# Four steps instead of three per mLSTM chunk: where the state's product and the output's norm stand

## The chip, the cores and the metric

One core of a Trainium2 chip. The time is the device time of one execution in microseconds; a version is timed in several runs and the median counts. One further execution is recorded by the hardware profiler, and all rows come from it. Engines: PE (TensorE, matmul and transpose), DVE (VectorE), ACT (ScalarE), POOL (GpSimd), and SP, whose queue issues the DMAs.

## The reference, cut to what matters

A decoder layer over 1024 tokens: three token mixers on one normalised input, gates that merge them, an output projection, then a gated MLP. The change is in the second mixer, an mLSTM with 4 heads of 128, worked in 8 chunks of 128 tokens:

```python
def step(carry, inp):                       # one chunk, c_st and n_st carried
    ...
    s = jnp.einsum('bhtd,bhsd->bhts', qc, kc) * jnp.exp(log_d - m_t[..., None])
    num = s @ vc + w_inter * (c_st @ qc)    # written as einsums
    den = jnp.sum(s, axis=-1) + w_inter * (n_st @ qc)
    h = num / jnp.maximum(jnp.abs(den), jnp.exp(-m_t))
    c_new = decay * c_st + einsum('bhs,bhsv,bhsk->bhvk', wk, vc, kc)
    n_new = decay * n_st + einsum('bhs,bhsk->bhk', wk, kc)
# then per head: y_ml = sigmoid(ml_o) * rmsnorm(h) * ml_g_out
```

All values are float32.

## The kernel before, in words

Most of the time is dense projections in three matmuls of split float32 (`mm3`, L149 to L151), 128x512 each. In the stretch of the change the dense work is a list of units (`seven`, L679), each with two weight pages: the first from the tag `raw` (L688, 2 buffers), the second from the tag `pg` (L691). The tag `pg` has 16 pages; 12 of them hold the split inputs `gd` that every unit reads (L761), which leaves 4. `go(1)` (L929) lets the dense list advance by one piece. The pieces go round: the start of a new unit (24 matmuls), the end of the one before (24), the middle of the new one (36).

The mLSTM chunks are worked between those pieces. `ml_chunk(g, c, state)` (L841) does one chunk for two heads (`g` is 0 or 1) and is a generator whose `yield`s mark its steps. In the loop over chunks (L947) each turn takes the first step of both groups of the new chunk, one dense piece, the last step of the old chunk and the second step of the new one, and another dense piece.

- First step: loads of q, k and v into `y` (L846, L850), of the output gate `og` (L852), of the gate rows `me` (L855); the causal mask on POOL (L858); the exponentials `dt_` on ACT (L864) and the scaled queries `qt` on POOL (L865); scores `pz` on PE (L868), multiplied into `dt_` on DVE (L869); k transposed on PE into `pk` (L874) and scaled on DVE into `kw` (L877); and the state's product `pst` = kw x v on PE (L880).
- Second step: numerators and denominators `pn` on PE (L887, L888), the state's update on DVE (L896), the denominators on DVE (L903 to L906), the numerators divided on ACT into `hm`, which is the first half of the tile `me` (L911), their squares (L913), and the norm: L155 on DVE, a power on POOL (L157), L916 on DVE.
- Third step: transposes `py` on PE (L920), the output gate on DVE (L922), the store (L923).

Buffers: `me` and `y` have 2, `mw` (og, dt_, qt, kw, yn) has 8. The PSUM tags `tr` (pk, pn, py) and `z` (pz, pst) have 2 banks each; the dense work uses two other tags in this stretch.

The order on each engine, SP's queue included, is fixed before the run by a planner: the place in the program is the priority, and among what its own estimate of times holds to be ready, the earliest goes first. Each engine then works its list in order and waits where a result or a buffer is late.

Of the kernel before, what the change touches and what calls it, by code (L numbers as in the profile page):

```python
# [12 lines left out]
AF = mybir.ActivationFunctionType  # L13
ALU = mybir.AluOpType
# [4 lines left out]
P = 128  # L19
# [23 lines left out]
def tile_hybrid_layer(ctx: ExitStack, tc: tile.TileContext, xT, memT, vecs, w_t, w_n, w_kv, w_if,  # L43
# [4 lines left out]
    nc = tc.nc  # L48
# [19 lines left out]
    def T(shape, tag, dt=F32, bufs=None):  # L68
        pool = {"mw": mlp, "mst": mlp, "ga": mlp, "gm": mlp,  "px": late[0]}.get(tag, sb)
        return pool.tile(shape, dt, tag=tag, name=nm(tag), bufs=bufs or BUFS[tag])  # L70

    def page(tag="pg", dt=F32):
        return T([P, S], tag, dt)
# [15 lines left out]
    def bank(tag):  # L89
        if tag in ("pj", "pv"):  # L90
            return ps.tile([P, HALF], F32, tag=tag, name=nm("ps_" + tag), bufs=2)
        if px1 is not None:
            if not spare.get(tag):
                t = two(tag)
                spare[tag] = [t[:, 1], t[:, 0]]
            return spare[tag].pop()
        return psx[0].tile([P, HALF], F32, tag=tag, name=nm("ps_" + tag), bufs=2)
# [7 lines left out]
    def ts(t):  # L105
        return slice(t * P, (t + 1) * P)
# [6 lines left out]
    ident = ident_r.bitcast(F32)  # L113
# [724 lines left out]

        return seven(w_t[T_MLO + j], w_t[T_MLO + j + 1], gx, done)

    def ml_chunk(g, c, state):  # L841
        hd = (2 * g, 2 * g + 1)
        qv = T([P, 4 * P + 258], "y")
        qk = qv[:, :4 * P].rearrange("p (i h t) -> p i h t", i=2, h=2)
        for i in range(2):
            nc.sync.dma_start(qk[:, i], qk_d[4 * i + 2 * g:4 * i + 2 * g + 2, :, ts(c)].rearrange("h p t -> p h t"))  # L846
        q, k = qk[:, 0], qk[:, 1]
        vx = qv[:, 4 * P:].rearrange("p (h v) -> p h v", h=2)
        nc.gpsimd.memset(vx[:, :, 128:129], 1.0)
        nc.sync.dma_start(vx[:, :, :P], v_d[c, :, 256 * g:256 * g + 256].rearrange("p (h v) -> p h v", h=2))  # L850
        og = T([P, 2, P], "mw")
        nc.sync.dma_start(og, o_d[2 * g:2 * g + 2, :, ts(c)].rearrange("h p t -> p h t"))  # L852
        me = T([P, 2, 2, P], "me")
        for i in range(2):
            nc.sync.dma_start(me[:, i].rearrange("p h t -> p (h t)"),  # L855
                              me_d[i, 4 * c + 2 * g:4 * c + 2 * g + 2].rearrange("h t -> (h t)")
                              .partition_broadcast(P))
        nc.gpsimd.affine_select(out=me[:, 0], in_=me[:, 0], pattern=[[0, 2], [-1, P]], compare_op=ALU.is_ge,  # L858
                                fill=-1e30, base=0, channel_multiplier=1)
        dt_ = T([P, 2, P], "mw")  # L860
        qt = T([P, 2, P], "mw")
        for i, h in enumerate(hd):
            r = 4 * c + h
            nc.scalar.activation(dt_[:, i], me[:, 0, i], AF.Exp, bias=cols[:, 0, r:r + 1])  # L864
            nc.gpsimd.tensor_mul(qt[:, i], q[:, i], me[:, 1, i])  # L865
        pz = bank("z")
        for i in range(2):
            nc.tensor.matmul(pz[:, ts(i)], k[:, i], q[:, i], start=True, stop=True)  # L868
        nc.vector.tensor_mul(dt_.rearrange("p h t -> p (h t)"), dt_.rearrange("p h t -> p (h t)"), pz[:, :2 * P])  # L869
        if c > 0:  # L870
            kw = T([P, 2, P], "mw")
            pk = bank("tr")
            for i, h in enumerate(hd):
                nc.tensor.transpose(pk[:, ts(i)], k[:, i], ident)  # L874
            for i, h in enumerate(hd):
                r = 4 * c + h
                nc.vector.tensor_scalar(kw[:, i], pk[:, ts(i)], cols[:, 1, r:r + 1], None, op0=ALU.mult)  # L877
            pst = bank("z")
            for i, h in enumerate(hd):
                nc.tensor.matmul(pst[:, i * 129:(i + 1) * 129], kw[:, i], vx[:, i], start=True, stop=True)  # L880
        yield
        pn = bank("tr")
        first = state[0] is None
        for i, h in enumerate(hd):
            o_ = pn[:, i * 129:(i + 1) * 129]
            if not first:
                nc.tensor.matmul(o_, qt[:, i], state[0][:, i], start=True, stop=False)  # L887
            nc.tensor.matmul(o_, dt_[:, i], vx[:, i], start=first, stop=True)  # L888
        if c > 0:
            new = T([P, 2, 129], "mst", bufs=2) if first else state[0]  # L890
            for i in range(2):
                s_ = pst[:, i * 129:(i + 1) * 129]
                if first:
                    nc.vector.tensor_copy(new[:, i], s_)
                else:
                    nc.vector.scalar_tensor_tensor(new[:, i], new[:, i], me[:, 1, i, 0:1], s_,  # L896
                                                   op0=ALU.mult, op1=ALU.add)
            state[0] = new

        pn2 = pn[:, :258].rearrange("p (h v) -> p h v", h=2)  # L900
        rd = small(2)
        r0 = 4 * c + 2 * g
        nc.vector.scalar_tensor_tensor(rd, pn2[:, :, 128], -1.0, cols[:, 2, r0:r0 + 2],  # L903
                                       op0=ALU.mult, op1=ALU.max)
        nc.vector.tensor_tensor(rd, rd, pn2[:, :, 128], op=ALU.max)
        nc.vector.reciprocal(rd, rd)  # L906
        ss = small(2)
        yn = T([P, 2, P], "mw")
        hm = me[:, 0]
        for i in range(2):  # L910
            nc.scalar.activation(hm[:, i], pn2[:, i, :P], AF.Copy, scale=rd[:, i:i + 1])  # L911
        for i in range(2):
            nc.scalar.activation(yn[:, i], hm[:, i], AF.Square, accum_out=ss[:, i:i + 1])  # L913
        rr = rstd_cols(ss, 2, MLD)
        for i in range(2):
            nc.vector.tensor_scalar(yn[:, i], hm[:, i], rr[:, i:i + 1], None, op0=ALU.mult)  # L916
        yield
        py = bank("tr")
        for i in range(2):
            nc.tensor.transpose(py[:, ts(i)], yn[:, i], ident)  # L920
        for i, h in enumerate(hd):
            nc.vector.scalar_tensor_tensor(og[:, i], py[:, ts(i)], col(C_GOUT + h), og[:, i], op0=ALU.mult, op1=ALU.mult)  # L922
        nc.sync.dma_start(y_d[1][2 * g:2 * g + 2, :, ts(c)].rearrange("h p t -> p h t"), og)  # L923
        yield
# [18 lines left out]
    next(rows_step)  # L943
    go(12)
    state = [[None], [None]]
    old = []
    for c in range(NCH - 1, -1, -1):  # L947
        new = [ml_chunk(g, c, state[g]) for g in range(2)]
        for u in new:
            next(u)  # L950
        go(1)
        for u in old:
            next(u)
        for u in new:
            next(u)
        go(1)
        old = new
    for u in old:
        next(u)


    def xa_attn(h):
# [67 lines left out]
    for i in range(3 * KT):  # L1030
        b, n = i // KT, i % KT
# [371 lines left out]
```

## Time and profile before

| | us |
|---|---|
| median of 3 runs | 1709.09 |
| lowest, highest | 1708.9, 1711.78 |
| the profiled execution | 1707.22 |
| its span in the trace | 1705.4 |

The profiled execution is 1.87 us below the median. Between its time and its span lie 1.8 us that the trace does not cover. PE is busy for 1666.4 us of the span. Idle time of an engine counts only where nothing else fills the span, so here the idle time of PE is what to look at, and in the stretch of the chunks above all.

### The profile page before, as it was taken

The numbers are of one execution on the slowest core, as the hardware profiler recorded it, in microseconds if no ns is written. First come the engines' busy times: TensorE is split into PE (matmuls) and PEld (weight loads), VectorE is DVE, ScalarE is ACT, GpSimd is POOL, SyncE is SP. The second block draws the span as 40 slices with busy tenths as digits, with TensorE's granted clock in tenths as the row PEclk, the third lists the DMA queues.
The fourth block names the chain that finished last, engine by engine and source line by source line (L and its number), as shares of the span: only waits on it lengthen the run. The fifth ranks groups of instructions, "written<-read, shape, count | busy, mean of one in ns | idle before, by whom it ended". The sixth has DMA issues, their size and how long they took to land.

```text
span 1705.4 us, 21424 instructions
## 1 busy us (share of the span) xinstructions
PE 1666.4 (98%) x7927; PEld 1334.5 (78%) x7927; DVE 1195.2 (70%) x1752; ACT 824.4 (48%) x1293; POOL 72.0 (4%) x149
## 2 busy tenths in 40 slices
PE   8999999999999999999999999999999999999999
PEld 4777777787777777777787888688888888788887
DVE  5558777678945555555457747997877787689874
ACT  4547667545544444555412324465554555543531
POOL 1000000020000222100000000000000000000000
PEclk9999999999999999999999999999999999999999
DMA  8321011233323545432666255142222222486042
GB/s 297 139 64 32 26 38 56 98 114 123 125 105 130 166 151 177 155 99 93 236 202 187 88 194 204 32 142 74 75 100 86 75 75 72 145 338 227 30 144 76
DMA packets 99069, 212.73 MB, mean 125 GB/s; under 512 B 13184, under 2 KB 41088, under 8 KB 98964
## 3 DMA queue, kind: packets, MB, share of 16 engines
q1 hardware_dynamic: 98964, 211.35, 36.5%
q8 instruction: 63, 1.03, 0.3%
q14 instruction: 42, 0.34, 0.1%
HBM read 156.71 MB, written 54.61 MB: 124 GB/s over the span
## 4 chain that ended last, share of the span: by engine, by line
PE 58%; DMA 2%; DVE 2%; ACT 2%; issue 1%; POOL 0%; POOLq 0%; SPq 0%; ACTq 0%; DVEq 0%
PE ps_pj L149 8%; PE ps_pj L151 8%; PE ps_pj L150 8%; PE ps_pv L150 4%; PE ps_pv L149 4%; PE ps_pv L151 4%; PE ps_tr L149 3%; PE ps_tr L150 3%; PE ps_tr L151 3%; PE ps_z L150 2%; PE ps_z L149 2%; PE ps_z L151 2%; DMA raw<-y_d 1%; PE ps_z L1003 1%; PE ps_z L978 1%
## 5 line engine op out<-in xcount | busy, mean ns | idle before, releaser
L150 PE MATMUL ps_pj<-h,whi 128*128 128x512 f32 x620 | 243.4, 393 | 0.0
L136 ACT ACTIVATE whi<-raw 128x512 fp32r<-128x512 f32 (+1 forms) x112 | 93.6, 836 | 189.2 <-PE ps_pj L150 86.2
L149 PE MATMUL ps_pj<-h,whi 128*128 128x512 f32 x412 | 163.4, 397 | 0.7 <-DVE U L1046 0.7
L149 PE MATMUL ps_pj<-pg,whi 128*128 128x512 f32 x396 | 155.2, 392 | 0.1
L151 PE MATMUL ps_pj<-pg,wlo 128*128 128x512 f32 x380 | 148.3, 390 | 0.2 <-DVE wlo L137 0.2
L150 PEld LDWEIGHTS ps_pj<-h,whi 128*128 128x128 f32 x620 | 116.5, 188 | 24.5 <-issue 1.0
L151 PE MATMUL ps_pj<-h,wlo 128*128 128x512 f32 x332 | 131.3, 395 | 0.7 <-DVE wlo L137 0.7
L816 DVE SCALAR_TENSOR_TENSOR y<-U,vec,y 128x1023 f32<-128x1023 f32 x88 | 112.4, 1279 | 8.0 <-ACT y L814 8.0
L422 DVE TENSOR_TENSOR_SCAN U<-U 128x512 f32<-128x512 f32 (+3 forms) x96 | 88.6, 964 | 31.3 <-ACT U L415 30.4
L149 PEld LDWEIGHTS ps_pj<-h,whi 128*128 128x128 f32 x412 | 77.4, 188 | 17.0 <-DVE U L1046 1.5
L137 DVE TENSOR_TENSOR wlo<-raw,whi 128x1024 fp32r<-128x1024 f32 x54 | 66.0, 1222 | 33.5 <-ACT whi L136 33.5
L149 PEld LDWEIGHTS ps_pj<-pg,whi 128*128 128x128 f32 x396 | 74.3, 188 | 17.3 <-issue 1.6
L151 PEld LDWEIGHTS ps_pj<-pg,wlo 128*128 128x128 f32 x380 | 71.3, 188 | 15.6 <-DVE wlo L137 0.6
L136 ACT ACTIVATE whi<-pg 128x512 fp32r<-128x512 f32 (+1 forms) x59 | 43.4, 737 | 75.1 <-PE ps_pv L150 20.1
L151 PEld LDWEIGHTS ps_pj<-h,wlo 128*128 128x128 f32 x332 | 62.6, 189 | 15.1 <-DVE wlo L137 1.6
L150 PE MATMUL ps_pj<-pg,whi 128*128 128x512 f32 x188 | 74.4, 396 | 0.0
L137 DVE TENSOR_TENSOR whi<-raw,whi 128x512 fp32r<-128x512 f32 x58 | 40.1, 691 | 35.7 <-ACT whi L136 35.6
L150 PE MATMUL ps_pv<-h,whi 128*128 128x512 f32 x164 | 63.8, 389 | 0.0
L814 ACT ACTIVATE y<-U,vec 128x1024 f32<-128x1024 f32 x44 | 54.6, 1241 | 14.5 <-DVE U L720 14.4
L151 PE MATMUL ps_pj<-h,whi 128*128 128x512 f32 x156 | 61.4, 393 | 0.0
L436 ACT ACTIVATE y<-ps_tr 128x1024 f32<-128x1024 f32 (+3 forms) x48 | 39.0, 813 | 39.0 <-PE ps_tr L434 38.7
L137 DVE TENSOR_TENSOR wlo<-raw,wlo 128x512 fp32r<-128x512 f32 x58 | 40.0, 690 | 24.1 <-ACT wlo L136 23.9
(429 smaller groups left out, 4328.0 us busy)
## 6 DMA issues: line engine op xcount, KB each, us to landing
raw<-in_w_t_dram SPq DMA_DIRECT2D x29, 512.0 KB, 4.4
gate_d<-U SPq DMA_DIRECT2D x24, 512.0 KB, 3.2
U<-gate_d SPq DMA_DIRECT2D x24, 512.0 KB, 3.8
pg<-in_w_up_dram SPq DMA_DIRECT2D x22, 512.0 KB, 4.0
act_d<-y SPq DMA_DIRECT2D x22, 512.0 KB
pg<-in_w_t_dram SPq DMA_DIRECT2D x21, 512.0 KB, 3.6
raw<-in_w_dn_dram SPq DMA_DIRECT2D x18, 512.0 KB, 4.7
raw<-in_w_o_dram SPq DMA_DIRECT2D x16, 512.0 KB, 3.4
```

Source lines behind the costliest of these rows:

```text
L136: nc.scalar.activation(hi, src, AF.Copy)
L137: (eng or nc.vector).tensor_sub(lo, src, hi.bitcast(F32))
L149: nc.tensor.matmul(out, lh, rh, start=start, stop=False, skip_group_check=more)
L150: nc.tensor.matmul(out, lh, rl, start=False, stop=False, skip_group_check=more)
L151: nc.tensor.matmul(out, ll, rh, start=False, stop=stop, skip_group_check=more)
L422: nc.vector.tensor_tensor_scan(f[:, a, 1:w + 1], f[:, a, 1:w + 1], f[:, a, 1:w + 1], 1.0 if o == 0 else f[:, a, 0:1], op0=ALU.mult, op1=AL ...
L436: nc.scalar.activation(wt[:, :, :w], pt[:, :, :w], AF.Copy)
L814: nc.scalar.activation(out, u, AF.Identity, bias=bias, scale=taps[0])
L816: nc.vector.scalar_tensor_tensor(out[:, :S - s], u[:, s:], taps[s], out[:, :S - s], op0=ALU.mult, op1=ALU.add)
L978: nc.tensor.matmul(z[:, i * NMEM:(i + 1) * NMEM], q[:, ts(2 * t2 + i)], kv[:, 0], start=True, stop=True)
L1003: nc.tensor.matmul(pv, kv[:, 1, ts(m)], pTs[m], start=(m == 0), stop=(m == 1))
```

## The change: what it does

- The state's product (`pst`, L878 to L880) moves from the first step into the second, behind `pn` and ahead of the state's update.
- The second step ends behind the squares. The norm (L155, L157, L916) becomes a third step, taken after the first step of the next chunk and before the dense piece that follows it. Transposes, output gate and store are the fourth step, where the third stood.
- One page of the tag `pg`, `kept`, is taken for the whole loop. It holds `kw` and `hm` of both groups. `hm` is no longer in `me`, `kw` no longer in `mw`; the normed output is written over `hm` and needs no `yn`; the squares go to `qt`.
- The load of `og` moves from the first step to the end of the second.

```diff
-    def ml_chunk(g, c, state):
+    def ml_chunk(g, c, state, hm, kw):
...
-        og = T([P, 2, P], "mw")
-        nc.sync.dma_start(og, o_d[2 * g:2 * g + 2, :, ts(c)].rearrange("h p t -> p h t"))
...
-            kw = T([P, 2, P], "mw")
             pk = bank("tr")
...
-            pst = bank("z")
-            for i, h in enumerate(hd):
-                nc.tensor.matmul(pst[:, i * 129:(i + 1) * 129], kw[:, i], vx[:, i], start=True, stop=True)
         yield
         pn = bank("tr")
...
         if c > 0:
+            pst = bank("z")
+            for i, h in enumerate(hd):
+                nc.tensor.matmul(pst[:, i * 129:(i + 1) * 129], kw[:, i], vx[:, i], start=True, stop=True)
...
-        yn = T([P, 2, P], "mw")
-        hm = me[:, 0]
         for i in range(2):
             nc.scalar.activation(hm[:, i], pn2[:, i, :P], AF.Copy, scale=rd[:, i:i + 1])
         for i in range(2):
-            nc.scalar.activation(yn[:, i], hm[:, i], AF.Square, accum_out=ss[:, i:i + 1])
+            nc.scalar.activation(qt[:, i], hm[:, i], AF.Square, accum_out=ss[:, i:i + 1])
+        og = T([P, 2, P], "mw")
+        nc.sync.dma_start(og, o_d[2 * g:2 * g + 2, :, ts(c)].rearrange("h p t -> p h t"))
+        yield
         rr = rstd_cols(ss, 2, MLD)
         for i in range(2):
-            nc.vector.tensor_scalar(yn[:, i], hm[:, i], rr[:, i:i + 1], None, op0=ALU.mult)
+            nc.vector.tensor_scalar(hm[:, i], hm[:, i], rr[:, i:i + 1], None, op0=ALU.mult)
         yield
...
+    kept = page().rearrange("p (n h t) -> p n h t", n=4, h=2)
...
     for c in range(NCH - 1, -1, -1):
-        new = [ml_chunk(g, c, state[g]) for g in range(2)]
-        for u in new:
-            next(u)
+        new = [ml_chunk(g, c, state[g], kept[:, g], kept[:, 2 + g]) for g in range(2)]
+        steps(new)
+        steps(old)
         go(1)
-        for u in old:
-            next(u)
-        for u in new:
-            next(u)
+        steps(old)
+        steps(new)
         go(1)
         old = new
-    for u in old:
-        next(u)
+    steps(old)
+    steps(old)
```

## Rows read from the trace of the kernel before

**Rows 1.** The page: the span, and PE's busy time, share of the span and number of instructions.

```profile
span 1705.4 us, 21424 instructions
...
PE 1666.4 (98%) x7927; PEld 1334.5 (78%) x7927; DVE 1195.2 (70%) x1752; ACT 824.4 (48%) x1293; POOL 72.0 (4%) x149
```

**Rows 2.** Windows of the span: from and to, length, then busy time (and number) of PE, PEld, DVE, ACT and POOL, the granted clock of PE, the DMA share and GB/s. The first is the stretch of the chunks, the second dense work behind it, the third lies within the first.

```profile
535.00:704.00 169.00, 157.83 (x820) 128.80 (x819) 98.88 (x292) 80.16 (x215) 34.92 (x73) 0.99 0.53 163
740.00:800.00 60.00, 59.93 (x264) 47.01 (x263) 31.46 (x68) 32.48 (x66) 3.27 (x2) 1.00 0.29 97
...
620.00:624.40 4.40, 4.06 (x15) 3.57 (x16) 1.69 (x4) 0.00 (x0) 0.74 (x2) 0.61 0.37 126
```

**Rows 3.** Waits of PE between 530 and 700 us: who waited, for whom, total us, times, longest.

```profile
PE ps_z L880 <- POOL mw L865: 1.9, 1, 1.9
PE ps_z L868 <- PE ps_pj L151: 1.7, 2, 0.9
PE ps_tr L874 <- ACT whi L136: 1.5, 1, 1.5
PE ps_z L880 <- issue: 1.4, 3, 0.8
PE ps_tr L874 <- ACT me L911: 1.4, 2, 0.8
PE ps_z L868 <- issue: 1.1, 2, 0.6
PE ps_tr L920 <- DVE mw L916: 1.1, 1, 1.1
PE ps_tr L874 <- DMA y<-qk_d: 0.5, 1, 0.5
...
PE ps_tr L920 <- DVE mw L922: 0.3, 1, 0.3
```

**Rows 4.** The timeline of all engines between 589.5 and 602.6 us, one turn of the chunk loop (start, us, engine, line, output and input, count, and the idle time just before with what ended it).

```profile
590.94 0.60 DVE L896 SCALAR_TENSOR_TENSOR mst<-mst,me,ps_z 128x129 f32<-128x129 f32 x2
...
593.30 0.33 DVE L896 SCALAR_TENSOR_TENSOR mst<-mst,me,ps_z 128x129 f32<-128x129 f32 x1
...
595.22 0.70 POOL L157 TENSOR_TENSOR sm<-sm,nhalf 128x2 f32<-128x2 f32 x1 [2.10 <-DVE sm L903]
595.96 0.48 DVE L916 TENSOR_SCALAR mw<-me,sm 128x128 f32<-128x128 f32 x2 [0.75 <-POOL sm L157]
596.36 0.15 DVE L905 TENSOR_TENSOR sm<-sm,ps_tr 128x2 f32<-128x2 f32 x1
596.50 0.81 SPq L855 DMA_DIRECT2D me<-me_d  x2
...
597.21 0.63 ACT L911 ACTIVATE me<-ps_tr,sm 128x128 f32<-128x128 f32 x2 [1.34 <-DVE sm L906]
597.89 0.44 PE L874 MATMUL ps_tr<-ident,y 128*128 128x128 f32 x2 [0.82 <-ACT me L911]
...
599.43 0.48 DVE L916 TENSOR_SCALAR mw<-me,sm 128x128 f32<-128x128 f32 x2 [0.81 <-POOL sm L157]
599.83 0.60 DVE L877 TENSOR_SCALAR mw<-ps_tr,cols 128x128 f32<-128x128 f32 x2
599.98 0.80 SPq L855 DMA_DIRECT2D me<-me_d  x2
600.13 0.41 POOL L858 TENSOR_SCALAR_AFFINE_SELECT me<-me 128x256 f32<-128x256 f32 x1 [0.73 <-DMA me<-me_d]
600.27 0.70 PE L880 MATMUL ps_z<-y,mw 128*128 128x129 f32 x4 [0.32 <-issue]
600.58 0.69 ACT L864 ACTIVATE mw<-me,cols 128x128 f32<-128x128 f32 x2 [2.16 <-POOL me L858]
...
601.30 0.42 DVE L869 TENSOR_TENSOR mw<-mw,ps_z 128x256 f32<-128x256 f32 x1 [0.87 <-ACT mw L864]
...
601.82 0.68 PE L868 MATMUL ps_z<-y 128*128 128x128 f32 x4 [0.61 <-issue]
```

**Rows 5.** Waits of the other engines and of SP's queue in the same stretch: who waited, for whom, total us, times, longest.

```profile
POOL mw L865 <- PE ps_tr L920: 26.1, 7, 7.8
...
POOL me L858 <- DMA me<-me_d: 17.8, 13, 4.4
...
DVE mw L916 <- POOL sm L157: 12.5, 16, 0.8
...
SPq L855 <- DVE mw L916: 16.6, 12, 2.1
```

**Rows 6.** One piece of the chain that ended last (start, us, what): a load of q and k.

```profile
634.31 3.60 DMA y<-qk_d
```

**Rows 7.** The timeline of SP and DVE: three loads of a unit's second weight page, and the first use of one.

```profile
561.89 0.42 SPq L691 DMA_DIRECT2D pg<-in_w_t_dram  x1
...
566.01 0.69 DVE L701 TENSOR_TENSOR hf<-pg 128x512 f32<-128x512 f32 x1 [0.88 <-DMA pg<-in_w_t_dram]
...
589.93 0.35 SPq L691 DMA_DIRECT2D pg<-in_w_t_dram  x1
...
622.20 0.42 SPq L691 DMA_DIRECT2D pg<-in_w_t_dram  x1
```

More of the change, by code (lines that the diff above doesn't have):

```diff
@@ L919, in ml_chunk @@
         for i in range(2):
-            nc.tensor.transpose(py[:, ts(i)], yn[:, i], ident)
+            nc.tensor.transpose(py[:, ts(i)], hm[:, i], ident)
         for i, h in enumerate(hd):
@@ L945, in tile_hybrid_layer, with steps @@
     state = [[None], [None]]
+    kept = page().rearrange("p (n h t) -> p n h t", n=4, h=2)
     old = []
+    def steps(units):
+        for u in units:
+            next(u)
     for c in range(NCH - 1, -1, -1):
-        new = [ml_chunk(g, c, state[g]) for g in range(2)]
-        for u in new:
-            next(u)
+        new = [ml_chunk(g, c, state[g], kept[:, g], kept[:, 2 + g]) for g in range(2)]
+        steps(new)
+        steps(old)
         go(1)
-        for u in old:
-            next(u)
-        for u in new:
-            next(u)
+        steps(old)
+        steps(new)
         go(1)
         old = new
-    for u in old:
-        next(u)
+    steps(old)
+    steps(old)
     def xa_attn(h):
```

## The prediction, made before the changed kernel was run

> **What bounds the kernel now.** I read the page first, then the windows of the stretch that the change touches, then PE's waits there, and last one turn of the chunk loop engine by engine.
>
> The page shows PE busy for 1666.4 of 1705.4 us [rows 1]: the kernel runs at PE's pace, and only time in which PE stands still, or runs slowly, can be won. The windows say where that is. Dense work behind the chunks leaves PE 0.07 us idle in 60; the 169 us of the chunks leave 169.00 - 157.83 = 11.2 us [rows 2]. Within them one short window has a granted clock of 0.61, that is, part of it at the lower level of 1.2 GHz instead of 2.4. PE's waits name 10.9 us of the 11.2 [rows 3]; the rest I leave alone.
>
> Sorted by place, the waits are: the state's product L880 and the scores L868, 1.9 + 1.7 + 1.4 + 1.1 = 6.1; the transposes of k, L874, behind ACT's L911, 1.4; other L874, 1.5 + 0.5 = 2.0; the transposes of the output, L920, 1.1 + 0.3 = 1.4.
>
> One turn of the loop shows how the first two arise [rows 4]. DVE's list has the norm of group 0 (L916, at 595.96, after 0.75 us of waiting for POOL's power) ahead of the denominators of group 1 (L905, 596.36). So ACT divides group 1's numerators only at 597.21, their `tr` bank comes free late, and PE's L874 has stood 0.82 us when it starts at 597.89. Since the numerators `hm` lie in `me`, the next `me` loads also wait for L916: they go out at 596.50 and 599.98. The first lands for POOL's mask at 600.13, ACT's exponentials follow at 600.58, DVE's L869 at 601.30, and only then is a `z` bank free for the scores of group 1, L868, at 601.82 with 0.61 us of standing. L880 meanwhile needs `kw`, whose L877 stands behind the second L916 (599.43) on DVE: 0.32 us.
>
> **The change part by part.** Nothing is added to the number of matmuls, vector, scalar or POOL instructions or DMAs; all of it is place and buffers. So the sum is over PE's waits.
>
> *The product leaves the first step, the norm leaves the second.* In the first step the two `z` banks now serve the two score products alone; L868 of group 1 no longer needs L869 of group 0. L880 stands behind L888, which needs the same `dt_` and comes a whole dense piece later, so `kw` is long there. The whole 6.1 us can go. What could be late next is L888 itself, waiting for `dt_` and `qt`. From the last state update of a chunk to L888 of the next: two issues of 0.4, 3.6 for the load (596.50 to 600.13), 0.4 for the mask, 0.7 for the exponentials, 0.4 for L869, with 0.9 more for the second group's load and its queue: 6.8 us [rows 4]. Between the two stand two dense pieces; one matmul costs 59.93 / 264 = 0.227 us [rows 2], so 24 + 24 give 10.9 us and 24 + 36 give 13.6. The slack is at least 4 us, above the longest PE wait of 1.9 in rows 3.
>
> *`hm` leaves `me`.* The load of `me` needs L896 instead of L916. Group 0's update ended at 591.54 and its load went out at 596.50; group 1's at 593.63 and 599.98 [rows 4]. The loads can be 5.0 and 6.4 us earlier, less some 0.5 and 0.9 for the products that now precede the update (L880 is 0.70 long for both heads, largely overlapped). This is the cover for the line above. SP's own 16.6 us of waiting at L855 [rows 5] go with it, and what is queued behind it on SP (the q, k and `og` loads) moves up.
>
> *Order on DVE.* Group 1's denominators come ahead of group 0's L916, so L905 can start some 2 us earlier, right behind its inputs, and the bank of L911 comes free that much earlier: the 1.4 us of L874 go.
>
> *Clock.* The one window below full clock starts with PE idle before L880, the longest wait of rows 3. At 0.61 over 4.40 us it lost 4.40 x 0.39 = 1.7 us [rows 2]. If that wait goes I expect the dip to go: 1.7. Lower bound 0, if another pause sets it off.
>
> *Other L874 and L920.* The 0.5 us waited for a q and k load of 3.6 us [rows 3, 6]. `y` is still freed by the second step's matmuls (now L880 instead of L888), so its time to the next first step is still one dense piece, 5.4 or 8.2 us, against two issues of 0.4 and 3.6. The 1.5 us has a releaser that I cannot tie to a moved step. I take half of the 2.0: 1.0. Of L920's 1.4, the 1.1 is the very last chunk, with nothing behind it to wait on but the norm; group 1's earlier denominators help there. I take half: 0.7.
>
> *Buffers and `og`.* Both groups used ten `mw` tiles a chunk out of eight; now six. POOL's 26.1 us at L865 [rows 5], waiting for a transpose to give its buffer back, go; POOL is off the path, so I cost this at nothing. It would cost only through `qt`, which the slack of 4 us covers. The 16 `og` loads are as many as before and are needed a dense piece and a first step later: at least 5.4 us for a load of about 3.6, if it takes what `me` takes. Without that cover each would cost up to 3.6.
>
> *New waits.* Rows of before cannot show them. Bounds: 0, and 6.1 (all of L880's and L868's standing reappears at L888). I take the smallest kind of wait that the planner's misjudgement leaves now, 0.3 us [rows 3], once per chunk: 2.4.
>
> **Sum.** 6.1 + 1.4 + 1.7 + 1.0 + 0.7 - 2.4 = 8.5 us. From the profiled execution: 1707.2 - 8.5 = 1698.7. It lay 1.9 below the median of the runs, so I forecast a median of 1700.6. All the waits and the dip gone would be 10.9 + 1.7 = 12.6: 1696.5.
>
> **The rivals.**
>
> *Half of the gain.* If the weight loads and not the matmuls set PE's pace, the room is smaller than the gaps: the loads are busy 128.80 of 169 us here and 47.01 of 60 in the dense work [rows 2]; at that dense share the stretch would still take 128.80 / 0.7835 = 164.4 us, a gain of 4.6 at most: 1704.5. For it: the chunk's small matmuls carry a weight load each, as the large ones do. Against it: each gap has a named place and a wait. Chance 0.15. The Trainium skill, "Perfetto Trace Analysis", section "Identifying the Most-Contended Engine", holds matmul busy time for a bad measure of the room, since matmuls are pipelined, and asks for the weight loads' share instead. [...]
>
> *The waits only move.* The planner issues what its estimate calls ready; if the loads of `me` are longer than it thinks, L888 stands where L868 stood, 6.1 us come back, and 8.5 + 2.4 - 6.1 = 4.8, less the dip if the pause remains, leaves 3.1: 1706.0. Against it: the slack of 4 us. Chance 0.11; the effect counts as no change.
>
> *POOL holds VectorE (slower).* The norm now stands behind the next first step in the program, so the planner may put POOL's power L157 behind the mask L858. L858 waits for its load for up to 4.4 us, 17.8 in all; L916 then waits on DVE, which already stands there 16 times [rows 5], and the splits of the dense weights are queued behind it. If each of the 16 powers is late by 1.4 us, the mean of those waits (17.8 / 13), and PE feels all of it, 22 us come on top of the sum: 1722.6. It decides from 0.75 us each on: 16 x 0.75 is 12, which eats the 8.5 and the 3.4 beyond it that can be told from nothing. For it: the queue on POOL is in order. Against: after the squares the power is ready some 3 us behind the state's update, the load only 4 to 5 us behind it. Chance 0.08.
>
> *The page.* Of four free `pg` pages one is taken. The second weight page of a unit is loaded when an older unit's is split, at 561.89, 589.93, 622.20, once in some 30 us [rows 7], and used 4.1 us later by DVE (566.01), a piece or more ahead of PE. With three pages this moves back by one unit, and two units are open at a time. If a unit did wait for its load, 4.1 us for each of some six units cost 25 us: 1725. It decides only if three units hold their pages at once. Chance 0.06.
>
> **How the numbers follow.** The forecast has 0.60. About 0.2% (3.4 us) is what a measurement of this kernel can tell from no change. Faster: 0.60 + 0.15 + a little of the moved waits, 0.77. Same: most of the moved waits and mild forms of the slower cases, 0.14. Slower: 0.09. The range goes from all waits gone, 1696.5, with half a us of spread, to just beyond the moved waits, 1707.5; the slower cases are left out.
>
> **What the profile would show.** Right: no L880 or L868 among PE's waits; L855 waiting for L896 or nothing; L905 of group 1 ahead of L916 of group 0; no window below full clock in the stretch; the 169 us at about 160. Wrong: PE waiting at L887 or L888 for L865 or L869; L157 behind L858 on POOL; L702 or L701 waiting for `pg` loads just before PE stands.

## The result and the profile after

| | before | after |
|---|---|---|
| median, us | 1709.62 (1708.9 to 1711.78, 4 runs) | 1700.26 (1699.57 to 1701.33, 4 runs) |
| ratio, 95% interval | | 0.9944 [0.9926, 0.9961] |
| profiled execution, us | 1707.22 | 1701.33 |
| its span | 1705.4 | 1699.6 |

The change wins 0.56%, between 0.39 and 0.74%. The two profiled executions are only 5.9 us apart: that of before was faster than its four timed runs, that of after is the slowest of its four. A second timing of the changed kernel (e0_after, below) gave 1697.98 us and 0.993 [0.9913, 0.9946].

The page after, span and PE, beside [rows 1]: the same 7927 matmuls are busy 2.2 us less.

```profile
span 1699.6 us, 21431 instructions
...
PE 1664.2 (98%) x7927; PEld 1337.9 (79%) x7927; DVE 1196.2 (70%) x1752; ACT 823.8 (48%) x1293; POOL 71.5 (4%) x149
```

The windows, beside [rows 2]: the stretch of the chunks, and the place within it where the granted clock is low.

```profile
535.00:694.00 159.00, 152.57 (x810) 129.61 (x809) 99.75 (x292) 78.24 (x210) 34.57 (x75) 0.99 0.59 180
...
652.00:656.00 4.00, 4.00 (x15) 3.18 (x14) 2.73 (x8) 0.69 (x2) 1.28 (x3) 0.57 0.57 196
```

PE's waits between 530 and 700 us, beside [rows 3]. Lines have moved: the scores L868 are now L866, k's transposes L874 are L871, the numerators L887 and L888 are L881 and L882, the product L880 is L886, the output's transposes L920 are L918, the mask L858 is L856, the norm L916 is L914, `me`'s load L855 is L853.

```profile
PE ps_z L866 <- DMA y<-qk_d: 6.2, 4, 2.7
PE ps_pj L149 <- ACT U L707: 0.2, 1, 0.2
```

Every wait of [rows 3] has gone but that for a load of q and k, which has grown from 0.5 us (at L874) to 6.2 (at the scores). Waits of the other engines in the same stretch, beside [rows 5]:

```profile
POOL me L856 <- DMA me<-me_d: 28.4, 14, 4.6
...
DVE pg L914 <- POOL sm L157: 23.9, 16, 3.9
```

POOL's 26.1 us at the scaled queries behind a transpose are gone, and SP's 16.6 us at `me` behind the norm too. The norm on DVE now waits for POOL's power up to 3.9 us at a time instead of 0.8. The timeline of SP's queue, POOL, DVE and PE around one of the new waits shows both late things:

```profile
621.71 2.30 SPq L846 DMA_DIRECT2D y<-qk_d  x2
624.10 0.42 SPq L850 DMA_DIRECT2D y<-v_d  x1
...
624.61 0.89 SPq L853 DMA_DIRECT2D me<-me_d  x2
...
625.59 0.90 SPq L846 DMA_DIRECT2D y<-qk_d  x2
...
627.61 0.60 PE L866 MATMUL ps_z<-y 128*128 128x128 f32 x4
628.55 0.41 POOL L856 TENSOR_SCALAR_AFFINE_SELECT me<-me 128x256 f32<-128x256 f32 x1 [3.33 <-DMA me<-me_d]
628.93 0.70 POOL L157 TENSOR_TENSOR sm<-sm,nhalf 128x2 f32<-128x2 f32 x1
...
629.66 0.89 DVE L914 TENSOR_SCALAR pg<-pg,sm 128x128 f32<-128x128 f32 x2 [3.84 <-POOL sm L157]
630.36 0.68 PE L866 MATMUL ps_z<-y 128*128 128x128 f32 x4 [1.92 <-DMA y<-qk_d]
```

Group 1's q and k are issued at 625.59, behind group 0's q, k, v and `me`, which take SP's queue from 621.71. PE can start on them only 4.8 us later, 2.75 us after group 0's scores began. Meanwhile POOL's mask stands for `me` until 628.55, the power is queued behind it, and DVE stands 3.84 us for the power.

To weigh the stretch as a whole I took the time from the first scores to the first product of the attention behind (L1003 before, L1005 after). Each kernel issues 481 dense matmuls in it, so the lengths can be compared. PE's idle time in it is the sum of the idle times that the timeline's rows show; the rest is the difference.

| kernel | from, to | length, us | PE idle | gaps | rest |
|---|---|---|---|---|---|
| before | 539.7, 703.9 | 164.2 | 10.9 | 14 | 153.3 |
| after | 541.2, 697.0 | 155.8 | 6.4 | 5 | 149.4 |
| d1_product_alone | 540.8, 691.5 | 150.7 | 2.9 | 3 | 147.8 |
| g2_qk_ahead | 540.0, 687.1 | 147.1 | 0.2 | 1 | 146.9 |
| e1_product_back | 541.7, 716.2 | 174.5 | 17.4 | 12 | 157.1 |

The change saves 8.4 us in its stretch, 4.5 of them idle time and 3.9 in "busy" time. The whole span is only 5.8 us shorter, since after reaches the stretch 1.5 us later and takes 1.1 us longer behind it.

A part of the rest is the clock. The windows of the same stretches, first e1_product_back, then b1_buffers_only, then d1_product_alone:

```profile
541.70:716.20 174.50, 157.10 (x798) 130.96 (x796) 100.08 (x290) 77.30 (x207) 32.47 (x72) 0.94 0.52 159
...
539.80:712.10 172.30, 156.41 (x799) 130.65 (x797) 98.17 (x290) 77.52 (x207) 33.58 (x72) 0.95 0.54 161
...
540.80:691.50 150.70, 147.65 (x799) 125.25 (x797) 98.03 (x290) 78.03 (x209) 35.20 (x73) 1.00 0.60 180
```

A granted clock of 0.94 over 174.5 us is a loss of some 10 us, beside 1.7 in the stretch of each of the kernels before and after (one dip each) and none in d1_product_alone. So a long wait of PE can be paid twice, standing and then at the lower clock: in e1_product_back the clock is 0.59 from 642 to 650 us, around waits that end at 641.80 (3.04 us) and 645.01 (2.35 us). Not each one is: the wait of 3.42 us in h1_product_back_ahead that ends at 579.71 has no dip behind it.

### The profile page after: what moved, and what is told of

It is laid out like the page before. It is cut to its first block, busy times and chain, and to the rows that moved or that the text cites. A ratio compares the mean times of both kernels' runs of the same rounds, so it can differ in the third digit from the quotient of the medians.

```text
span 1699.6 us, 21431 instructions
## 1 busy us (share of the span) xinstructions
PE 1664.2 (98%) x7927; PEld 1337.9 (79%) x7927; DVE 1196.2 (70%) x1752; ACT 823.8 (48%) x1293; POOL 71.5 (4%) x149
## 4 chain that ended last, share of the span: by engine, by line
PE 86%; ACT 4%; DVE 4%; DMA 3%; issue 2%; SPq 1%; POOL 0%; POOLq 0%; ACTq 0%; DVEq 0%
PE ps_pj L149 14%; PE ps_pj L150 13%; PE ps_pj L151 13%; PE ps_pv L150 6%; PE ps_pv L151 6%; PE ps_pv L149 6%; PE ps_tr L149 4%; PE ps_tr L150 4%; PE ps_tr L151 4%; PE ps_z L151 2%; PE ps_z L150 2%; PE ps_z L149 2%; PE ps_pv L448 2%; PE ps_tr L434 2%; DMA y<-qk_d 1%
## 5 line engine op out<-in xcount | busy, mean ns | idle before, releaser
L149 PE MATMUL ps_pj<-h,whi 128*128 128x512 f32 x412 | 163.6, 397 | 0.8 <-DVE U L1048 0.8
L149 PE MATMUL ps_pj<-pg,whi 128*128 128x512 f32 x396 | 155.3, 392 | 0.2 <-DVE pg L1046 0.2
L149 PEld LDWEIGHTS ps_pj<-h,whi 128*128 128x128 f32 x412 | 77.9, 189 | 16.6 <-DVE U L1048 1.2
L149 PEld LDWEIGHTS ps_pj<-pg,whi 128*128 128x128 f32 x396 | 74.4, 188 | 17.6 <-issue 1.6
L151 PE MATMUL ps_tr<-pg,wlo 128*128 128x512 f32 x144 | 56.1, 389 | 0.0
```

The source lines that it names most:

```text
L149: nc.tensor.matmul(out, lh, rh, start=start, stop=False, skip_group_check=more)
L151: nc.tensor.matmul(out, ll, rh, start=False, stop=stop, skip_group_check=more)
```

## The experiments

All kernels but m1_switch were timed in five rounds beside the kernel before on the same chip; the ratio is to that.

| kernel | median, us | ratio, 95% interval |
|---|---|---|
| e0_after | 1697.98 | 0.993 [0.9913, 0.9946] |
| e1_product_back | 1717.31 | 1.0045 [1.0028, 1.0061] |
| e2_norm_back | 1699.28 | 0.9939 [0.9922, 0.9955] |
| b1_buffers_only | 1714.77 | 1.0037 [1.0024, 1.005] |
| d1_product_alone | 1694.27 | 0.9923 [0.9906, 0.9939] |
| f2_me_act | 1696.45 | 0.9925 [0.9911, 0.9938] |
| g1_qk_merged | 1690.75 | 0.9902 [0.9886, 0.9918] |
| g2_qk_ahead | 1691.32 | 0.9899 [0.9885, 0.9912] |
| h1_product_back_ahead | 1716.43 | 1.005 [1.0037, 1.0062] |
| h3_norm_back_ahead | 1716.28 | 1.0047 [1.0033, 1.006] |
| k1_me_ahead | 1718.1 | 1.007 [1.005, 1.009] |

### Which part pays

**e0_after** is the changed kernel again, as a measure for the other kernels.

> The changed kernel again, in more rounds. If the two profiles are typical (1707.22 and 1701.33 us), the gain is nearer 6 us, about 1703 beside 1709; if the medians are, it is 9.4 us, ratio 0.9945, about 1700. PE's waits in the chunk stretch (about 535 to 700 us) should again be the loads of q and k, near 6 us, and nothing else.

It came to 1697.98 us with a span of 1696.3, against 1699.6 in the first profile. PE waits 6.3 us for the loads of q and k, again four times, and the stretch takes 155.9 us. Both reach L1005 for the last time at 819.3 us, so the 3.3 us between the two profiles arise behind the chunks. The window from 830 us shows where, first in the first profile of the changed kernel:

```profile
830.00:840.00 10.00, 10.00 (x39) 8.04 (x38) 4.20 (x5) 4.73 (x5) 0.00 (x0) 0.83 0.76 259
```

and then in e0_after:

```profile
830.00:840.00 10.00, 10.00 (x46) 8.27 (x45) 4.51 (x5) 4.62 (x5) 0.00 (x0) 1.00 0.90 314
```

One has a granted clock of 0.83, the other 1.00: 1.7 us; about another 1.0 us is idle time of PE between 820 and 830. Both differ between two executions of the same kernel, so neither belongs to the change.

**e1_product_back**: the product in the first step again, the rest as changed.

```diff
                 nc.vector.tensor_scalar(kw[:, i], pk[:, ts(i)], cols[:, 1, r:r + 1], None, op0=ALU.mult)
+            pst = bank("z")
+            for i, h in enumerate(hd):
+                nc.tensor.matmul(pst[:, i * 129:(i + 1) * 129], kw[:, i], vx[:, i], start=True, stop=True)
         yield
...
-            pst = bank("z")
-            for i, h in enumerate(hd):
-                nc.tensor.matmul(pst[:, i * 129:(i + 1) * 129], kw[:, i], vx[:, i], start=True, stop=True)
```

> The state's product goes back to the first step; all else as in the changed kernel. Theory A (the product's place sets PE's waits, since the two z banks then have to serve product and scores in one step): L880's and L868's standing comes back, near 6 us, and the median is 4 to 6 us above the changed kernel. Theory B (the late me loads set them, the product's place only shows where): with hm out of me the loads are early, so the product's place matters little: within 1.5 us of the changed kernel.

Its 1717.31 us are 19.3 more than the changed kernel and more than the kernel before: Theory A in direction and in the product's waits (6.4 us at L877), but over three times its size. The stretch is 18.7 us longer than the changed kernel's, 11.0 of them idle time; the lower clock covers the other 7.7. The largest of PE's waits is for q and k, at k's transposes:

```profile
DVE pg L914 <- POOL sm L157: 26.4, 16, 6.1
...
PE ps_tr L871 <- DMA y<-qk_d: 10.4, 5, 3.5
...
PE ps_z L877 <- POOL mw L863: 2.7, 2, 2.4
```

**e2_norm_back**: the norm at the end of the second step again, the rest as changed.

```diff
-        yield
         rr = rstd_cols(ss, 2, MLD)
         for i in range(2):
             nc.vector.tensor_scalar(hm[:, i], hm[:, i], rr[:, i:i + 1], None, op0=ALU.mult)
+        yield
         yield
```

> The norm goes back to the end of the second step (the third step is then empty); product, page and output gate as in the changed kernel. Theory A (the norm of group 0 stands ahead of group 1's denominators on DVE and holds a tr bank): 1 to 3 us slower than the changed kernel, with PE waiting at L871 for ACT. Theory B (the order on DVE is off the path once the loads of me no longer wait for the norm): within 1 us.

1699.28 us: 1.3 more than e0_after, with intervals that overlap almost wholly. The norm's own step is worth nothing that these runs can tell.

**b1_buffers_only**: the kernel before, with `hm` and `kw` in the page and the squares in `qt`; product, norm and `og` where they were.

```diff
-            kw = T([P, 2, P], "mw")
...
-        yn = T([P, 2, P], "mw")
-        hm = me[:, 0]
...
-            nc.scalar.activation(yn[:, i], hm[:, i], AF.Square, accum_out=ss[:, i:i + 1])
+            nc.scalar.activation(qt[:, i], hm[:, i], AF.Square, accum_out=ss[:, i:i + 1])
```

> Only the buffers of the change: hm and kw in the page, squares over qt; product in the first step, norm in the second, output gate loaded in the first, as before. Theory A (places): at most 3 us faster than before, L880 and L868 still among PE's waits. Theory B (loads of me): most of the gain, 6 us or more.

The freed buffers make the kernel slower than before by 0.24 to 0.5%. So the theory that most of the gain comes from loading `me` early falls. The stretch is 8.1 us longer than before: PE's idle time grows by some 5 us, and a clock of 0.95 costs some 8.6 us in place of 1.7. The waits:

```profile
DVE pg L913 <- POOL sm L157: 22.5, 16, 4.6
...
PE ps_tr L873 <- DMA y<-qk_d: 10.2, 4, 3.7
PE ps_tr L873 <- ACT wlo L136: 2.6, 1, 2.6
```

**d1_product_alone**: the kernel before with the product in the second step and only `kw` in a page; `hm` stays in `me`.

```diff
-            kw = T([P, 2, P], "mw")
...
-            pst = bank("z")
-            for i, h in enumerate(hd):
-                nc.tensor.matmul(pst[:, i * 129:(i + 1) * 129], kw[:, i], vx[:, i], start=True, stop=True)
         yield
...
         if c > 0:
+            pst = bank("z")
+            for i, h in enumerate(hd):
+                nc.tensor.matmul(pst[:, i * 129:(i + 1) * 129], kw[:, i], vx[:, i], start=True, stop=True)
```

> The kernel before with one part of the change alone: the scaled k in a page and the state's product with the state's update moved into the second step; the o loads, the outputs hm and the norm stay as before. Theory P, the product's place is what pays: the waits at L880 and L874 (7.5 us in the kernel before) go and the time comes to 1698 to 1701, within 3 us of the whole change (1698.0). Rival, the product pays only together with the other buffers (the loads of me still wait for hm's last reader, the o loads still stand ahead of them on SyncE's queue): 1703 to 1708.

It beat the expectation: 1694.27 us. (The waits at L880 and L874 of [rows 3] come to 6.7 us, not 7.5.) The product's place alone, with the page for `kw`, gives the whole gain, and the other parts of the change added nothing. The ratio's interval overlaps that of the changed kernel, so that the other parts cost time isn't settled by the ratios; its stretch is 5.1 us shorter (150.7 against 155.8, and 155.9 in the second profile of the changed kernel): 3.5 us of idle time and a clock dip of 1.7. Its waits:

```profile
DVE mw L915 <- POOL sm L157: 11.8, 15, 0.8
...
PE ps_z L868 <- DVE wlo L137: 1.2, 1, 1.2
PE ps_tr L919 <- DVE mw L915: 1.1, 1, 1.1
```

No load of q and k is waited for. On SP's queue `me` goes out behind group 1's q and k here:

```profile
586.50 0.88 SPq L846 DMA_DIRECT2D y<-qk_d  x2
...
588.50 0.96 SPq L846 DMA_DIRECT2D y<-qk_d  x2
...
591.42 0.33 SPq L855 DMA_DIRECT2D me<-me_d  x1
...
625.11 0.93 SPq L846 DMA_DIRECT2D y<-qk_d  x2
...
628.02 0.68 PE L868 MATMUL ps_z<-y 128*128 128x128 f32 x4
```

The last two rows show that the order on the queue isn't all. Here the scores use group 1's q and k 2.9 us after the issue, without a wait; in the four turns of the changed kernel with a wait, 4.7 to 5.4 us pass. So there the transfers themselves take longer as well. That `me`'s transfers, on their way at the same time, are what slows them is likely but not shown by itself.

### The wait that is left: q and k of group 1

**f2_me_act**: the changed kernel with `me` issued from ScalarE's queue.

```diff
-            nc.sync.dma_start(me[:, i].rearrange("p h t -> p (h t)"),
+            nc.scalar.dma_start(me[:, i].rearrange("p h t -> p (h t)"),
```

> The changed kernel, with the two broadcast loads of me issued from ScalarE's queue instead of SyncE's. Theory C1: group 1's q and k are late because group 0's me loads (0.9 us for the pair) are issued ahead of them on SyncE's queue. Then L866's wait falls from 6.3 us by 0.9 us at each of its four places, to 2.7 us, and the time by 3 to 5 us to 1693 to 1695. Rival C2, the loads wait for their buffer or for crowded transfers and not for the queue: the wait stays within 1.5 us of 6.3 and the time at 1697 to 1699. Rival, ScalarE pays: 28 or so issues in its queue push its exps and halves back, TensorE waits at L149 for ScalarE, 1700 or more.

PE's wait at L866 fell to 3.1 us in all (1.2 + 0.8 + 0.6 + 0.5), near the 2.7 expected, but the time, 1696.45, lies above the range expected, and its ratio can't be told from that of the changed kernel. So the two issues of `me` ahead on the queue account for about half of the wait. The largest two of what is left:

```profile
PE ps_z L866 <- DMA y<-qk_d: 1.2, 2, 0.7
PE ps_z L866 <- DMA me<-me_d: 0.8, 2, 0.6
```

**g2_qk_ahead**: q and k of both groups in one tile, filled by two transfers one chunk ahead; v in tiles of its own. **g1_qk_merged** is the same with the two transfers at the head of the chunk itself.

```diff
+    def ml_qk_load(c):
+        t = page("y").rearrange("p (i h t) -> p i h t", i=2, h=4)
+        for i in range(2):
+            nc.sync.dma_start(t[:, i], qk_d[4 * i:4 * i + 4, :, ts(c)].rearrange("h p t -> p h t"))
+        return t
...
-        qv = T([P, 4 * P + 258], "y")
...
+        q, k = qc[:, 0, 2 * g:2 * g + 2], qc[:, 1, 2 * g:2 * g + 2]
+        vx = T([P, 2, 129], "vx")
...
         steps(new)
+        ahead = ml_qk_load(c - 1) if c else None
```

> The changed kernel, with the q and k of both groups of a chunk in one tile that two transfers fill, issued one chunk ahead (v gets tiles of its own, the mw tiles are six instead of eight). Theory C: what the changed kernel still loses in the stretch is group 1's q and k, which land after the scores want them. Then the 6.3 us of TensorE's wait at L866 go, and the clock dip behind the longest of them: 6 to 9 us less than the changed kernel's 1698.0, so 1689 to 1692. Rival D, the next thing is as late (the broadcast loads of me, v, or a scarcer mw tile): the wait turns up at L867's readers, L881/L882 or L886, and the time is 1696 to 1699.

> The version with q and k ahead (1691.3), but with the two transfers issued at the head of the same chunk's first step instead of one chunk ahead. They no longer wait for a buffer, and both groups' q and k stand ahead of group 0's v and me on SyncE's queue. If the order on the queue and the buffer made them late: L866's counterpart waits under 1 us in all and the time is 1691 to 1693. If it was the time from issue to landing (3.3 us and more) after the chunk's begin: 3 to 6 us of wait stay, now at group 0's scores, and the time is 1694 to 1698.

1691.32 and 1690.75 us: some 7 us below the changed kernel's second timing, and the two agree. But they don't set loads at the chunk's head against loads ahead of it, for g1_qk_merged loads ahead too. These rows are its fifth chunk's first load of q and k, and that chunk's scores:

```profile
575.83 0.37 SPq L844 DMA_DIRECT2D y<-qk_d  x1
...
609.21 0.60 PE L868 MATMUL ps_z<-y 128*128 128x128 f32 x4
```

It goes out 33 us ahead, and in g2_qk_ahead the same load leaves at 575.5 us. The planner sends it as soon as the buffer is free. In the changed kernel the two tiles of `y` are one for each group and also hold v, so the second step of the chunk before frees them, and group 1's loads leave 4.7 to 6.9 us ahead of the scores from the second chunk on. In g1 and g2 the two tiles are one for each chunk, v lies elsewhere, and the first step of the chunk two before frees them. So the loads do wait for a buffer (SP's queue stands 17.6 us in all at L844 in g1_qk_merged, for L873 and L865), which the expectation ruled out, but early enough. What both kernels have and the changed one hasn't is the lead of some 30 us; whether two transfers instead of four matter by themselves was not tested. In g2_qk_ahead PE is busy throughout, at full clock:

```profile
600.00:620.00 20.00, 20.00 (x113) 17.26 (x113) 14.03 (x44) 8.35 (x26) 4.33 (x12) 1.00 0.62 185
...
640.00:660.00 20.00, 20.00 (x109) 17.09 (x108) 12.60 (x40) 10.57 (x33) 5.84 (x13) 1.00 0.68 205
```

These beat both kernels; nothing more is to be had from PE's waits in this stretch.

### Why the product's place counts for so much

**h1_product_back_ahead**: g2_qk_ahead with the product in the first step, by the same edit as in e1_product_back.

> The kernel in which the state's product was put back in the first step (1717.3), with q and k loaded one chunk ahead as in g2_qk_ahead. Theory C: that kernel's loss over the changed one (19.3 us) is mostly the same late load of q and k (10.4 us of wait at L871) and the clock that fell behind it; with the loads ahead it comes to 1700 to 1705, and what is left over g2_qk_ahead (some 6 us of waits at L877 and more switches) is the product's place. Rival E, the product's place by itself costs most of it: TensorE waits as long at L877 and the time stays at 1710 or above.

The wait for q and k is gone and the time hardly moved, 1716.43 us. The rival holds: another wait, larger than that one, takes its place.

```profile
PE ps_z L879 <- POOL mw L865: 16.1, 4, 4.4
```

The timeline of one of the four, all engines:

```profile
575.22 0.60 PE L873 MATMUL ps_tr<-ident,y 128*128 128x128 f32 x4
575.41 0.41 POOL L858 TENSOR_SCALAR_AFFINE_SELECT me<-me 128x256 f32<-128x256 f32 x1 [4.61 <-DMA me<-me_d]
575.78 0.70 POOL L157 TENSOR_TENSOR sm<-sm,nhalf 128x2 f32<-128x2 f32 x1
...
576.52 0.48 DVE L916 TENSOR_SCALAR pg<-pg,sm 128x128 f32<-128x128 f32 x2 [4.02 <-POOL sm L157]
577.16 0.70 POOL L157 TENSOR_TENSOR sm<-sm,nhalf 128x2 f32<-128x2 f32 x1 [0.67 <-DVE sm L155]
...
577.89 0.85 DVE L916 TENSOR_SCALAR pg<-pg,sm 128x128 f32<-128x128 f32 x2 [0.82 <-POOL sm L157]
...
579.26 0.34 DVE L876 TENSOR_SCALAR pg<-ps_tr,cols 128x128 f32<-128x128 f32 x1
...
579.71 0.46 PE L879 MATMUL ps_z<-vx,pg 128*128 128x129 f32 x2 [3.42 <-POOL mw L865]
```

The view names POOL's L865 as the releaser, but the product reads the scaled k (`pg`), and that ends on DVE at 579.60, 0.11 us before the product starts. DVE had k's transposes from about 575.8 on. It stood behind the norm (and 0.67 us of a dense sum, L720), the norm behind POOL's power, the power behind the mask, and the mask behind `me`. This is the chain of the rival "POOL holds VectorE".

**k1_me_ahead** meant to break it by issuing `me` after the second step of the chunk before, on top of h1_product_back_ahead.

```diff
         steps(new)
+        mes = [ml_me_load(g, c - 1) for g in range(2)] if c else None
         go(1)
```

> The kernel with the product back in the first step and q and k ahead (1716.4), with the loads of me issued ahead too, after the second step of the chunk before. Theory K: the product waits for the scaled k, which VectorE makes only after the norm's two scalings; those wait for POOL's power (L157), which stands on POOL's queue behind the mask that waits for me (me lands at 575.4, L157 575.8, the norm 576.5 and 577.9, the scaled k 579.3). With me early the 16.1 us of wait at L879 fall to under 5 us, and the time to 1694 to 1702. Rival, the wait is the product's own chain (scores, transposes, scaling, bank) whatever me does: the wait stays above 10 us and the time above 1708.

It settles nothing: the loads still went out behind the stores and v on SP's queue, at 569.54 us, only 1.7 us earlier than in h1_product_back_ahead (571.20). As PE is earlier by as much, they leave 3.6 us ahead of the scores in both kernels, and the mask still stood 4.82 us for them. DVE's hold stayed, up to 6.4 us, and so did the time.

```profile
569.54 1.84 SPq L850 DMA_DIRECT2D me<-me_d  x4
```

**h3_norm_back_ahead** moved the norm back to the end of the second step on top of h1_product_back_ahead, by the edit of e2_norm_back.

> The kernel with the product back in the first step and q and k ahead (1716.4), with the norm moved back to the end of the second step, so that VectorE's scaled k and POOL's mask no longer stand beside the norm's power and scalings of the chunk before. Theory K, the product in the first step is late because its scaled k stands on VectorE behind the norm's scalings, these behind POOL's power, and that behind the mask that waits for me: L879's wait of 16.1 us falls under 5 us and the time comes to 1692 to 1700. Rival, scores, transposes, scaling and product in one step are too long a chain whatever else stands there: L879's wait stays above 10 us and the time above 1706.

Theory K in that form falls: 1716.28 us, with as much waiting.

```profile
PE ps_z L879 <- POOL mw L865: 7.3, 2, 4.6
PE ps_z L868 <- DVE mw L869: 7.3, 2, 3.6
```

The norm's step is not what puts POOL's power behind the mask: with the norm back in the second step the longest hold of DVE is still 4.1 us. What does go with it, over the kernels run, is the place of `hm`:

| `hm` in | kernels | DVE's norm behind the power: total, longest, us |
|---|---|---|
| `me` | before; d1_product_alone | 12.5, 0.8; 11.8, 0.8 |
| the page, product in the first step | b1; e1; h1; h3; k1 | 22.5, 4.6; 26.4, 6.1; 25.6, 4.9; 25.8, 4.1; 27.2, 6.4 |
| the page, product in the second step | after; e0; e2; f2; g1; g2 | 23.9, 3.9; 25.1, 4.2; 25.8, 3.9; 30.8, 4.7; 22.0, 3.4; 22.7, 3.6 |

With `hm` in `me`, the next `me` can't be loaded until the norm has read `hm`, so a group's mask comes after its power on POOL; with `hm` in the page the planner can put it ahead. All five kernels with `hm` in the page and the product in the first step took 1714.8 to 1718.1 us, the ones with the product in the second 1690.8 to 1700.3. No kernel with the product in the first step had both the loads of q and k early and `hm` in `me`, so how the loss divides between the hold and those loads stays open. The clock has its part in it: in h1_product_back_ahead it is low in three places around waits of 3.9 to 4.4 us.

### What a switch between small and dense matmuls costs

In the stretch a dense matmul next to a small one starts its successor 0.31 to 0.32 us later instead of 0.227, and the change more than halves the switches between the kinds (118 to 50, both directions counted). **m1_switch** adds a stretch to the end of the changed kernel to price one; it was profiled once, and only that stretch is read.

```diff
+    big(192)
+    little(48)
+    for _ in range(48):
+        big(4)
+        little(1)
+    for _ in range(12):
+        big(16)
+        little(4)
```

> The changed kernel with an extra stretch at its end that waits for nothing: 192 dense matmuls (fp32r, 128x512), 48 small ones (fp32, 128x128), then 48 times four dense and one small, then 12 times sixteen dense and four small, then 64 dense. Theory S, a switch between the two kinds costs time of its own (in the stretch a dense matmul next to a small one took 0.31 to 0.32 us where others take 0.227): the stretch of 48 switches each way takes 4 to 9 us longer than the 192 dense and 48 small in two blocks, the stretch of 12 switches each way a quarter of that. Rival, the longer spacing came from operands that were not ready: the three stretches agree within 1 us.

The windows of the four parts: the two blocks, the stretch of 48 switches each way, that of 12.

```profile
1691.57:1735.10 43.53, 43.53 (x193) 36.04 (x192) 0.89 (x2) 0.00 (x0) 0.00 (x0) 1.00 0.06 22
1735.10:1745.74 10.64, 10.64 (x98) 10.63 (x96) 0.00 (x0) 0.00 (x0) 0.00 (x0) 1.00 0.01 2
1745.74:1800.79 55.05, 55.05 (x292) 46.85 (x290) 0.00 (x0) 0.00 (x0) 0.00 (x0) 1.00 0.00 1
1800.79:1855.20 54.41, 54.41 (x291) 46.76 (x290) 0.00 (x0) 0.00 (x0) 0.00 (x0) 1.00 0.00 1
```

In blocks the work takes 43.53 + 10.64 = 54.17 us, with 48 switches 55.05, with 12 switches 54.41. A switch there and back costs (55.05 - 54.17) / 48 = 0.018 us: the small matmul behind the dense one must give back most of what the dense one seems to lose. Theory S falls, since 34 pairs of switches fewer are worth 0.6 us.

## Why the prediction was right, and where its sum was wrong

The forecast was 1700.6 us, and 1700.26 were measured. The stretch gave 8.4 us where the sum had 8.5. But several terms were wrong and cancelled, so that it came so close is luck:

| term | sum | measured in the stretch | by |
|---|---|---|---|
| waits of L880 and L868 that were named | 6.1 | 6.1 | none left but for q and k |
| L874 behind L911 | 1.4 | 1.4 | gone, by another cause |
| other L874, L920 | 1.0 + 0.7 | 2.0 + 1.4 | gone |
| new waits | -2.4 | -6.4 | L866, 6.2; L149, 0.2 |
| the clock's dip | 1.7 | about 0 | another at 652 us |
| time counted as busy | 0 | 3.9 | rest, 153.3 to 149.4 |

**The product leaves the first step.** Right: no wait at the product or the numerators, and d1_product_alone shows that this move alone does it. The slack reckoned for the numerators (at least 4 us) held even with `me` landing late.

**`hm` leaves `me`.** This step failed. It said that what is queued behind L855 on SP "(the q, k and `og` loads) moves up". The early `me` loads moved up themselves, ahead of group 1's q and k: compare 624.61 and 625.59 after with 588.50 and 591.42 in d1_product_alone. The step counted two issues of 0.4 us and 3.6 for the load of q and k. After, there stand 2.30 + 0.42 + 0.89 + 0.90 of issues from group 0's load to the end of group 1's, and from the issue of group 1's to their first use pass 4.7 to 5.4 us where PE waits. f2_me_act, which takes `me` off this queue, halves the wait; g1_qk_merged and g2_qk_ahead, whose loads leave some 30 us ahead, end it.

**Order on DVE.** The 1.4 us went, but not by this step: in e2_norm_back group 0's norm (589.37) still stands ahead of group 1's denominators (589.77), and k's transposes wait for nothing there. They went with the product's move (d1_product_alone has no such wait either); by which link, no run separates.

**New waits.** Mis-sized and misplaced: 6.4 us at L866, above the upper bound of 6.1 and not at L888. The bound from the waits of before couldn't hold a load that was hardly late then.

**Clock.** The old dip went, as predicted, and another took its place: right behind the longest new wait (2.7 us, until 651.55) the granted clock is 0.57 over 652 to 656 us, a loss of 4 x 0.43 = 1.7 us, as much as in [rows 2]. d1_product_alone and g2_qk_ahead have none in their stretch. The lower bound, "if another pause sets it off", is what came.

**Other L874 and L920.** All 3.4 us went where half was taken.

**Time counted as busy.** The sum had no such term. The matmul ahead of a gap counts as busy 0.15 to 0.26 us beyond the spacing that matmuls of its kind have where nothing waits; over the 14 gaps of before these tails make 2.7 us, over the 5 of after 0.8. (The profile models the ends of matmuls, so this is a reading of its rows.) With 0.6 us for the switches that is 2.5 of the 3.9; the clock has no part in it, as both stretches lose 1.7, and about 1.4 us I can't assign.

**The rivals.** *Half of the gain* fell: it saw no stretch below 164.4 us, a gain of at most 4.6 in the windows of [rows 2], while the stretch gained 8.4 with this change and 17.1 in g2_qk_ahead. There the weight loads are busy 17.26 of 20 us, 86%, above the 78% of the dense work that it took for the ceiling. The Trainium skill, "Perfetto Trace Analysis", section "Identifying the Most-Contended Engine", asks for the matmuls' share of peak FLOPs beside the weight loads' share, and sets no such ceiling; the 78% was the prediction's own step. That busy time misleads, as it says, the trace bears out: 3.9 of the 8.4 us won were counted as busy. *POOL holds VectorE* happened as a mechanism: the power is behind the mask, and DVE's longest stand went from 0.8 to 3.9 us. PE felt none of it, because the numerators and the product come a dense piece later; the first-step kernels show it on the path. *The waits only move* came true in size, 6.2 us, but at the scores, for q and k, and not at L888 for `me`; the other waits that went paid for it. *The page* cost nothing: no PE wait for a weight load in the stretch.

**The signs.** Seen: no L880 or L868 waits of the old kind; SP no longer waiting for the norm; group 1's denominators ahead of group 0's norm (588.88 and 590.18); a stretch 8.4 us shorter, where the step from 169 to about 160 stood. Not seen as said: there is a window below full clock in the stretch. And one listed as wrong, the power behind the mask, appeared without harm.

## What to carry to other kernels

Ask of a buffer freed early not only who starts sooner but what that start is queued ahead of: here the early loads of `me` went ahead of the loads that PE needed next, and the mask ahead of the power. A product placed in the step after the one that makes its operand turns a chain over three engines into slack; try that single move before the rest of a change. When all waits on a busy engine have one name, ask what holds that load's buffer: two tiles that hold one chunk each, and not one group each, let q and k leave some 30 us ahead instead of about 5, in both kernels that gained another 7 us. And look behind a long wait for the clock: in e1_product_back 17.4 us of idle time came with a loss of some 10 us to the lower clock.

## What the runs showed of the hardware that was not expected

- A switch between a dense fp32r matmul of 128x512 and a small float32 one costs 0.018 us there and back, though the rows around it look 0.08 to 0.09 us longer each time.
- PE's busy time hides 0.15 to 0.26 us ahead of each gap, so a stretch with many gaps gains more than its idle time when they go: before to g2_qk_ahead, 10.7 us of idle time and 6.4 of "busy" time, of which 2.5 are such tails and 1.7 the clock.
- Two issues of q and k on SP's queue took 2.30 us at 621.71 and 0.90 at 625.59: one of the first two took 1.89 us, the other three 0.36 to 0.46.
- The same two loads of q and k (128 KB each) were in use 2.9 us after their issue in one kernel and 4.7 to 5.4 us after it in another, with the broadcast loads of `me` issued just ahead of them.
